# Rope's cosine product on VectorE from PSUM, its closing sum and a softmax subtraction on GpSimd

## The chip, the cores and the metric

The kernel runs on one core of a Trainium2 chip. A core has five engines that take their instructions in order and work beside each other: TensorE (PE in the profile) multiplies matrices from SBUF into PSUM, VectorE (DVE), ScalarE (ACT) and GpSimd (POOL) work on tiles, and SyncE (SP) issues most transfers. They wait for each other by semaphores. The metric is the device time of one execution in microseconds, the median over several runs. Lower is better.

## The reference, cut to what matters

One layer of a decoder trunk with 512 tokens of width 1024. After a norm, one projection gives the inputs of a pooling mixer and of a sparse attention with 16 heads; both are gated, merged and projected, and an MLP of width 4096 follows. Two pieces of the attention are touched here:

```python
def apply_rope(x, cos, sin):
    x1, x2 = jnp.split(x, 2, axis=-1)
    rot = jnp.concatenate([-x2, x1], axis=-1)
    y = x.astype(jnp.float32) * cos[:, None, :] + rot.astype(jnp.float32) * sin[:, None, :]
    return y.astype(x.dtype)
...
    q = apply_rope(q.reshape(B, S, N_HEADS, dh), cos, sin).reshape(B, S, G, HPG, dh)
    ks = apply_rope(ks.reshape(B, S, G, dh), cos, sin)
    kw = apply_rope(kw.reshape(B, S, G, dh), cos, sin)
...
        s_c = jnp.einsum('bqghd,bngd->bghqn', qb, k_cmp) * scale
        p_c = masked_softmax(s_c, cmp_end[None, :] <= t[:, None])
        o_c = jnp.einsum('bghqn,bngd->bqghd', p_c, v_cmp)
```

The first turns pairs of channels by an angle that grows with the position. The second is the softmax over 31 compressed keys for each query, one of three branches of the attention. The other two go over all earlier keys; with 512 tokens every block is picked and the window holds all of them, so both are causal softmaxes over the same positions with different keys and values.

## The kernel before, in words

All matrix products split each float32 operand into a high part and a remainder, and run three products (high by high, high by low, low by high). So every weight that arrives is split: ScalarE writes the high part (line 345), VectorE or, for the second half of a weight in the attention stage, GpSimd subtracts it from the raw weight (line 347).

The work falls into three stages: the projections with the pooling mixer and the compression of keys and values; the attention; and the output projection with the MLP, whose products are made with fewer multiplications by sums of quarters of the weights. Those sums are made by transfers which GpSimd issues (line 267, `S<-w_ff`).

**Rope** (`rope`, line 606) is called ten times: for the two keys (`ks`, `kw`) and for the queries of eight pairs of heads (`q0` to `q7`). ScalarE copies the projected tile from PSUM to `rx` with a scale (line 612). Four transfers on SyncE's queue write `rx` to `rs` with each pair of 32 partitions exchanged (615). Then `rx` is multiplied in place by the cosines in two halves (620), `rs` by the sines in two halves (623), and the two are added into `rx` (628). In the first stage, which holds the keys and q0 to q2, VectorE does all six; in the attention stage (`mode["pool"]`) GpSimd does the four products of q3 to q7 and VectorE the two sums. What follows makes the split operands, for a query in `q_done` (lines 653 to 658). `rope` is a generator: at each `yield` other work is emitted, so the number of yields says how many slots later the next instruction comes.

**The attention** goes pair by pair. A pair has twelve slots; each is one block of scores for one head (half 0: both branches for 128 or 256 positions; half 1: one branch, 384 or 512). For a slot, PE makes scores (`psS`, 1007), VectorE adds the mask, writes `P` and takes the minimum, since the scores are negated (1029), ScalarE takes the exponent with its sum (1039), VectorE inverts the sum (1049), GpSimd scales `P` by that and by the gate (1052), PE transposes `P` (`psT`, 1069), ScalarE and VectorE split the transposed tile (1080, 1084), and PE multiplies it with the values (`psO`, 1103). The transposes of a slot come four slots behind its scores, the product with the values two slots later still. Between slots PE runs filler, the remaining projections (`psF`, 388): q3 to q7 and the gate of the second mixer.

**The compressed branch** (`cmp_scores`, 939) runs as such a generator once for each pair, one pair ahead: scores (`psC`, 944), mask and sum of the two halves on VectorE (951, 952), the minimum (954), its subtraction (956), the exponent on ScalarE (959), the sum, its inverse and the gate on VectorE (961 to 964), then scaling and splitting on GpSimd (966 to 969), the transposes (977), and a copy by ScalarE (`pc`, 979) that PE multiplies into `psO` (1094).

The program text gives only the order of emission. A planner then orders the instructions of each engine by when it holds them to be ready; so instructions of later slots can stand ahead of earlier ones, and a changed instruction moves others.

Of the kernel before, what the change touches and what calls it, by code (L numbers as in the profile page):

```python
# [13 lines left out]
F32 = mybir.dt.float32  # L14
FR = mybir.dt.float32r
AF = mybir.ActivationFunctionType
ALU = mybir.AluOpType
# [3 lines left out]
S = 512  # L21
# [41 lines left out]
def trunk(ctx: ExitStack, tc: tile.TileContext, A, out):  # L63
    nc = tc.nc
    PE, ACT, DVE, POOL = nc.tensor, nc.scalar, nc.vector, nc.gpsimd
    PSUM = bass.MemoryType.PSUM

    def pool(name, **kw):
        return tc.tile_pool(name=name, bufs=1, reuse_waits="tile", **kw)
# [200 lines left out]
    mode = {"pool": False, "first": POOL}  # L270
# [202 lines left out]
    op = e2.enter_context(pool("op"))  # L473
# [3 lines left out]
    ap = at.enter_context(pool("att"))  # L477
# [86 lines left out]
    r, _ = evac0(1)  # L564
# [32 lines left out]
    cosT, sinT = cst[:, C_COS:C_COS + S], cst[:, C_SIN:C_SIN + S]  # L597
# [8 lines left out]
    def rope(ps, scale, done, after=0):  # L606

        assert not scored["rope"]
        scored["rope"] = 1
        xr = ap.tile([128, S], F32, tag="rx", bufs=1, name="rx")  # L610
        sw = ap.tile([128, S], F32, tag="rs", bufs=1, name="rs")
        ACT.activation(xr, ps, AF.Copy, scale=scale)
        for b in range(4):
            a = b ^ 1
            nc.sync.dma_start(sw[32 * b:32 * b + 32, :], xr[32 * a:32 * a + 32, :])
        yield
        eng = POOL if mode["pool"] else DVE
        hs = [slice(0, S // 2), slice(S // 2, S)]
        for c in hs:
            eng.tensor_tensor(xr[:, c], xr[:, c], cosT[:, c], op=ALU.mult)  # L620
            yield
        for c in hs:
            eng.tensor_tensor(sw[:, c], sw[:, c], sinT[:, c], op=ALU.mult)
            yield
        yield
        for c in hs:
            yield
            DVE.tensor_tensor(xr[:, c], xr[:, c], sw[:, c], op=ALU.add)
        while scored["pairs"] < after:
            yield  # L630
        for _ in done(xr):
            yield
        scored["rope"] = 0
# [250 lines left out]
    with ExitStack() as c2:  # L884
# [54 lines left out]
        def cmp_scores(p):  # L939
            g = p // 4  # L940
            ps = ps2.tile([128, NT, 2, 64], F32, tag="S", bufs=S_BANKS, name="psC")
            for qb in range(NT):
                for h in range(2):
                    PE.matmul(ps[:, qb, h, :], Q[p][:, h, 128 * qb:128 * qb + 128], KC[g], start=True, stop=True,
                              skip_group_check=True)
            w = p2.tile([128, NT, 2, 64], F32, tag="cw", bufs=1, name="cw")
            s8 = p2.tile([128, 3, 8], F32, tag="c8", bufs=1, name="c8")
            cm = cst[:, C_CM:C_CM + 128].rearrange("p (q n) -> p q n", q=NT)
            wl = w[:, :, :, 0:32]
            wf = w.rearrange("p q h n -> p (q h) n")[:, :, 0:32]  # L950
            DVE.tensor_tensor(wl, ps[:, :, :, 0:32], cm[:, :, None, :].to_broadcast([128, NT, 2, 32]), op=ALU.add)
            DVE.tensor_tensor(wl, ps[:, :, :, 32:64], wl, op=ALU.add)
            yield
            DVE.tensor_reduce(s8[:, 0, :], wf, axis=AX.X, op=ALU.min)
            yield
            DVE.tensor_tensor(wf, wf, s8[:, 0, :, None].to_broadcast([128, 8, 32]), op=ALU.subtract)
            yield
            yield
            ACT.activation(wl, wl, AF.Exp, scale=-1.0)
            yield  # L960
            DVE.tensor_reduce(s8[:, 1, :], wf, axis=AX.X, op=ALU.add)
            DVE.reciprocal(s8[:, 2, :], s8[:, 1, :])
            r = s8[:, 2, :].rearrange("p (q h) -> p q h", q=NT)
            DVE.tensor_tensor(r, r, GT[:, :, 6 * p:6 * p + 6:3], op=ALU.mult)
            yield
            POOL.tensor_tensor(wl, wl, r[:, :, :, None].to_broadcast([128, NT, 2, 32]), op=ALU.mult)
            pH, pL = (PC[:, :, e, :].rearrange("p q (h n) -> p q h n", h=2) for e in range(2))
            POOL.tensor_scalar(pH, wl, 1.0, 1.0, op0=ALU.mult, op1=ALU.mult)
            POOL.tensor_tensor(pL, wl, pH.bitcast(F32), op=ALU.subtract)
            yield  # L970
            yield
            yield
            yield
            pt = ps2.tile([128, S], F32, tag="T", bufs=T_BANKS, name="psT")
            for qb in range(NT):
                src = PC[:, qb, :, :].rearrange("p e c -> p (e c)")
                PE.transpose(pt[:, 128 * qb:128 * qb + 128].bitcast(FR), src, identR)
            t = p2.tile([128, S], FR, tag="pc", bufs=1, name="pc")
            ACT.activation(t, pt, AF.Copy)
            PTc[p] = t  # L980
# [126 lines left out]
        def o_evac(p, half):  # L1107
# [7 lines left out]
            split_ready()  # L1115

        side.append(cmp_scores(0))
        while 0 not in PTc:
            fill()
# [491 lines left out]
```

## Time and profile before

| | |
|---|---|
| median of 3 runs | 816.38 us (815.37 to 816.65) |
| the profiled execution | 815.44 us, of which 813.5 us are the span from the first to the last instruction |
| PE busy | 789.4 us, 97% of the span |
| DVE, ACT, POOL busy | 610.0 us, 484.8 us, 202.8 us |
| first stage | about 12 to 184 us of the span |
| attention | about 184 to 385 us |
| output projection and MLP | from there to the end |

A timeline row shows the start of an instruction or of a run of equal ones, how long it took, the engine, the line, the operation, the output and its inputs, how many there are (x4), and in brackets how long the engine stood idle before it and which instruction released it. A windows row shows a stretch of the span and the busy time of each engine in it with the number of instructions; PEclk is the share of its full clock that TensorE was granted. A row of groups shows busy time and the mean of one, then the idle time before them. A row of waits shows the total, the number and the longest.

### The profile page before, as it was taken

To read this page: it belongs to the slowest core of one execution; us is meant where nothing else is said; L and a number is where in the kernel's file an instruction comes from. 1 tells how busy PE (TensorE), PEld (TensorE's weight loads), DVE (VectorE), ACT (ScalarE), POOL (GpSimd) and SP (SyncE) were. 2 spreads that over 40 slices of the span, in tenths; PEclk is the share of its full clock that TensorE was granted. 3 is DMA by queue.
4 is the path that set the end of the run, shared out by engine and by line. 5 is a ranking of instruction groups with operands and counts; after the bars stand their busy time and mean duration, and the time that the engine had idled before them with its cause. 6 is when DMAs were issued, how large, how long until landed. Compare 5 with 4: busy or idle time off the path is not lost.

```text
span 813.5 us, 13961 instructions
## 1 busy us (share of the span) xinstructions
PE 789.4 (97%) x5091; PEld 707.8 (87%) x5091; DVE 610.0 (75%) x1199; ACT 484.8 (60%) x961; POOL 202.8 (25%) x269
## 2 busy tenths in 40 slices
PE   8999999998899999999999999999999999999996
PEld 7889878886788888888788899999999999999985
DVE  5796744539979898888565579996899689987823
ACT  6576533327787887899434475944773477346712
POOL 4000000027767867674334100111111100000000
PEclk9999999999999999999999999999999999999999
DMA  9564632357446634553964807999899955455402
GB/s 287 144 170 110 179 92 89 106 157 165 67 128 119 144 78 91 105 131 74 316 155 155 205 3 211 310 242 282 248 267 245 282 167 182 130 157 181 156 1 103
DMA packets 124445, 130.85 MB, mean 161 GB/s; under 512 B 5173, under 2 KB 112217, under 8 KB 124250
## 3 DMA queue, kind: packets, MB, share of 16 engines
q1 hardware_dynamic: 105082, 110.31, 42.6%
q0 software_dynamic: 19008, 18.88, 16.4%
q8 instruction: 40, 0.66, 0.3%
q10 hardware_dynamic: 288, 0.79, 0.3%
q14 instruction: 27, 0.22, 0.1%
HBM read 125.24 MB, written 39.85 MB: 203 GB/s over the span
## 4 chain that ended last, share of the span: by engine, by line
PE 74%; DVE 17%; ACT 4%; issue 3%; DMA 1%; POOL 0%; DVEq 0%; ACTq 0%; POOLq 0%
PE psF L388 22%; PE psB L388 15%; PE psB L1380 13%; PE psB L1496 8%; PE psO L1103 3%; PE psT L1069 3%; PE psS L1007 3%; DVE wl L302 2%; PE psV L388 2%; DVE P L1029 2%; DVE PT L1084 1%; PE psF L445 1%; DVE w3l L302 1%; DMA raw<-w_ff 1%; ACT P L1039 1%
## 5 line engine op out<-in xcount | busy, mean ns | idle before, releaser
L388 PE MATMUL psF<-R,wh 128*128 128x512 f32 x512 | 166.8, 404 | 0.9 <-ACT GB L682 0.6
L300 ACT ACTIVATE wh<-raw 128x1024 fp32r<-128x1024 f32 x66 | 69.8, 1057 | 75.5 <-PE psB L1496 33.4
L345 ACT ACTIVATE wh<-raw 128x512 fp32r<-128x512 f32 (+1 forms) x104 | 62.5, 619 | 84.6 <-PE psF L388 37.5
L388 PEld LDWEIGHTS psF<-R,wh 128*128 128x128 f32 x512 | 92.4, 189 | 18.7 <-ACT GB L682 0.8
L388 PE MATMUL psF<-R,wl 128*128 128x512 f32 x256 | 101.7, 397 | 0.8 <-DVE wl L347 0.8
L1052 POOL TENSOR_SCALAR P<-P,sm,GT 128x128 f32<-128x128 f32 (+3 forms) x128 | 86.0, 705 | 46.4 <-DVE sm L1049 32.2
L302 DVE TENSOR_TENSOR wl<-raw,wh 128x1024 fp32r<-128x1024 f32 x66 | 80.5, 1220 | 17.7 <-ACT wh L300 17.7
L267 POOL DMA_DIRECT2D S<-w_ff x36 | 41.8, 1160 | 191.9 <-DMA S<-w_ff 154.4
L347 DVE TENSOR_TENSOR wl<-raw,wh 128x512 fp32r<-128x512 f32 (+1 forms) x78 | 56.1, 732 | 33.1 <-ACT wh L345 32.7
L1039 ACT ACTIVATE P<-P,sm 128x128 f32<-128x128 f32 (+3 forms) x128 | 71.1, 557 | 11.7 <-DVE sm L1029 10.4
L1029 DVE CUSTOM_DVE_ANT_0 P<-psS,cst 128x128 f32<-128x128 f32 (+3 forms) x128 | 59.6, 483 | 6.2 <-PE psT L1069 4.6
L1380 PE MATMUL psB<-R,wh 128*128 128x256 f32 x352 | 64.1, 282 | 0.0
L347 POOL TENSOR_TENSOR wl<-raw,wh 128x512 fp32r<-128x512 f32 x28 | 39.0, 1398 | 87.5 <-ACT wh L345 85.2
L1084 DVE TENSOR_TENSOR PT<-psT,PT 128x512 fp32r<-128x512 f32 (+2 forms) x96 | 56.6, 594 | 4.1 <-ACT PT L1080 3.0
L388 PEld LDWEIGHTS psF<-R,wl 128*128 128x128 f32 x256 | 48.3, 188 | 11.9 <-DVE wl L347 0.9
L1080 ACT ACTIVATE PT<-psT 128x512 fp32r<-128x512 f32 (+2 forms) x96 | 49.2, 520 | 14.9 <-PE psT L1069 14.0
L1069 PE MATMUL psT<-ident,P 128*128 128x128 f32 x320 | 51.3, 275 | 6.3 <-POOL P L1052 5.0
L300 ACT ACTIVATE w3h<-raw 128x1024 fp32r<-128x1024 f32 x32 | 33.8, 1057 | 38.8 <-PE psB L1496 16.3
L1380 PEld LDWEIGHTS psB<-R,wh 128*128 128x128 f32 x352 | 54.1, 188 | 0.3 <-DVE R L1322 0.2
L1069 PEld LDWEIGHTS psT<-ident,P 128*128 128x128 f32 x320 | 39.6, 141 | 16.8 <-POOL P L1052 7.8
L1380 PE MATMUL psB<-R,wl 128*128 128x256 f32 x176 | 49.5, 281 | 0.0
L302 DVE TENSOR_TENSOR w3l<-raw,w3h 128x1024 fp32r<-128x1024 f32 x32 | 39.0, 1220 | 13.3 <-ACT w3h L300 13.3
(433 smaller groups left out, 2262.6 us busy)
## 6 DMA issues: line engine op xcount, KB each, us to landing
raw<-w_ff SPq DMA_DIRECT2D x56, 512.0 KB, 4.7
S<-w_ff POOLq DMA_DIRECT2D x36, 512.0 KB, 7.6
raw<-S SPq DMA_DIRECT2D x36, 512.0 KB, 5.1
raw<-w_in SPq DMA_DIRECT2D x32, 512.0 KB, 4.0
S<-w_ff SPq DMA_DIRECT2D x28, 512.0 KB, 5.3
S<-S SPq DMA_DIRECT2D x8, 512.0 KB, 7.0
raw<-w_proj_nsa SPq DMA_DIRECT2D x8, 512.0 KB, 4.1
raw<-w_out SPq DMA_DIRECT2D x8, 512.0 KB, 4.6
```

The costliest lines, as they stand in the source:

```text
L300: ACT.activation(h, t, AF.Copy)
L302: DVE.tensor_tensor(l, t, h.bitcast(F32), op=ALU.subtract)
L345: ACT.activation(h[:, sl], t[:, sl], AF.Copy)
L347: eng.tensor_tensor(l[:, sl], t[:, sl], h[:, sl].bitcast(F32), op=ALU.subtract)
L388: PE.matmul(ps, a, b, start=first and j == 0, stop=last and j == n - 1, skip_group_check=True)
L1029: DVE.tensor_tensor_reduce(out=P[:, o:o + n].rearrange("p (a c) -> p a c", c=128), in0=s, in1=m, scale=1.0, scalar=3e38, op0=ALU.add, op1= ...
L1039: last_exp[:] = [ACT.activation(c, c, AF.Exp, bias=sm[:, 0, e:e + 1], scale=-1.0, accum_out=sm[:, 1, e:e + 1])]
L1052: r = POOL.tensor_scalar(P[:, o:o + n], P[:, o:o + n], sm[:, 2, e:e + 1], GT[:, qb, c + e:c + e + 1], op0=ALU.mult, op1=ALU.mult)
L1069: PE.transpose(pt[:, 128 * j:128 * j + 128], P[:, 128 * j:128 * j + 128], ident)
L1084: DVE.tensor_tensor(dL, src, dH.bitcast(F32), op=ALU.subtract)
L1380: PE.matmul(out, w[u][:, k, 128 * f:128 * f + 128], XB[x][v][:, k, :], **kw)
L1496: PE.matmul(out, YB[y][u][:, k, 128 * f:128 * f + 128], w[v][:, k, :], **kw)
```

## The change

In `rope`, the cosine product becomes one instruction on VectorE over all 512 columns, which reads the projected tile in PSUM, scales it and multiplies by the cosines into a new tile `rc`. The sine products stay where they were. The closing sums go from VectorE to the engine of the products, which in the attention stage is GpSimd, and read `rc` instead of `rx`. The slots of the two cosine products stay as empty ones, one empty slot behind the sines goes, and in the attention stage three are added behind the sums. In `cmp_scores`, the subtraction of the minimum goes to GpSimd; two more slots follow it before the exponent, and one more follows the exponent.

```diff
@@ rope
         xr = ap.tile([128, S], F32, tag="rx", bufs=1, name="rx")
         sw = ap.tile([128, S], F32, tag="rs", bufs=1, name="rs")
+        xc = ap.tile([128, S], F32, tag="rc", bufs=1, name="rc")
         ACT.activation(xr, ps, AF.Copy, scale=scale)
         for b in range(4):
             a = b ^ 1
             nc.sync.dma_start(sw[32 * b:32 * b + 32, :], xr[32 * a:32 * a + 32, :])
+        DVE.scalar_tensor_tensor(xc, ps, scale, cosT, op0=ALU.mult, op1=ALU.mult)
         yield
         eng = POOL if mode["pool"] else DVE
         hs = [slice(0, S // 2), slice(S // 2, S)]
-        for c in hs:
-            eng.tensor_tensor(xr[:, c], xr[:, c], cosT[:, c], op=ALU.mult)
-            yield
+        yield
+        yield
         for c in hs:
             eng.tensor_tensor(sw[:, c], sw[:, c], sinT[:, c], op=ALU.mult)
             yield
-        yield
         for c in hs:
             yield
-            DVE.tensor_tensor(xr[:, c], xr[:, c], sw[:, c], op=ALU.add)
+            eng.tensor_tensor(xr[:, c], xc[:, c], sw[:, c], op=ALU.add)
+        if mode["pool"]:
+            for _ in range(3):
+                yield
@@ cmp_scores
             DVE.tensor_reduce(s8[:, 0, :], wf, axis=AX.X, op=ALU.min)
             yield
-            DVE.tensor_tensor(wf, wf, s8[:, 0, :, None].to_broadcast([128, 8, 32]), op=ALU.subtract)
-            yield
-            yield
+            POOL.tensor_tensor(wf, wf, s8[:, 0, :, None].to_broadcast([128, 8, 32]), op=ALU.subtract)
+            for _ in range(4):
+                yield
             ACT.activation(wl, wl, AF.Exp, scale=-1.0)
+            yield
             yield
             DVE.tensor_reduce(s8[:, 1, :], wf, axis=AX.X, op=ALU.add)
```

More of the change, by code (lines that the diff above doesn't have):

```diff
@@ L955, in cmp_scores @@
             yield
-            DVE.tensor_tensor(wf, wf, s8[:, 0, :, None].to_broadcast([128, 8, 32]), op=ALU.subtract)
+            POOL.tensor_tensor(wf, wf, s8[:, 0, :, None].to_broadcast([128, 8, 32]), op=ALU.subtract)
+            for _ in range(4):
+                yield
+            ACT.activation(wl, wl, AF.Exp, scale=-1.0)
             yield
-            yield
-            ACT.activation(wl, wl, AF.Exp, scale=-1.0)
             yield
```

## The prediction

> **What bounds the kernel now.** I read the shares of the engines first, then the busy times stage by stage, then whom PE waits for in the attention, and last the timelines around those waits.
>
> ```profile
> PE 789.4 (97%) x5091; PEld 707.8 (87%) x5091; DVE 610.0 (75%) x1199; ACT 484.8 (60%) x961; POOL 202.8 (25%) x269
> ```
>
> ```profile
> 20.00:184.00 164.00, 163.14 (x811) 136.47 (x810) 100.94 (x200) 77.26 (x144) 6.56 (x11) 1.00 0.48 132
> 184.00:220.00 36.00, 30.11 (x184) 24.84 (x183) 34.79 (x109) 28.31 (x84) 29.73 (x43) 0.97 0.64 124
> 220.00:380.00 160.00, 157.15 (x1005) 137.45 (x1004) 140.12 (x459) 133.09 (x357) 109.10 (x151) 1.00 0.48 105
> ```
>
> PE is the bound, so only PE's idle time and its clock can give a gain. The change adds no matmul. In the first stage PE stands idle 164.00 - 163.14 = 0.9 us; nothing is to be had there. In the first 36 us of the attention it is 5.9 us, and there DVE (34.79) and POOL (29.73) are nearly full. In the next 160 us it is 2.85 us. The views of waits and of PE's timeline name them:
>
> ```profile
> PE psT L1069 <- POOL P L1052: 5.0, 3, 2.4
> ...
> PE psF L388 <- DVE wl L347: 0.8, 1, 0.8
> ```
>
> ```profile
> 194.06 0.44 PE L1069 MATMUL psT<-ident,P 128*128 128x128 f32 x2 [2.17 <-POOL P L1052]
> 194.83 0.44 PE L1069 MATMUL psT<-ident,P 128*128 128x128 f32 x2 [0.33 <-POOL P L1052]
> ...
> 196.82 0.52 PE L1069 MATMUL psT<-ident,P 128*128 128x128 f32 x3 [0.62 <-DVE PT L1084]
> ...
> 217.52 1.21 PE L1069 MATMUL psT<-ident,P 128*128 128x128 f32 x4 [2.45 <-POOL P L1052]
> ```
>
> Two stalls of over 2 us, both of transposes that wait for a `P` scaled by GpSimd. GpSimd's timeline shows what stood ahead of that scaling:
>
> ```profile
> 190.30 1.83 POOL L620 TENSOR_TENSOR rx<-rx,cst 128x256 f32<-128x256 f32 x2
> 191.69 1.79 POOL L623 TENSOR_TENSOR rs<-rs,cst 128x256 f32<-128x256 f32 x2
> 193.08 2.31 POOL L1052 TENSOR_SCALAR P<-P,sm,GT 128x256 f32<-128x256 f32 x3
> ...
> 212.87 1.78 POOL L347 TENSOR_TENSOR wl<-raw,wh 128x512 fp32r<-128x512 f32 x1
> 214.14 1.88 POOL L620 TENSOR_TENSOR rx<-rx,cst 128x256 f32<-128x256 f32 x2
> 215.51 1.18 POOL L623 TENSOR_TENSOR rs<-rs,cst 128x256 f32<-128x256 f32 x1
> 216.22 1.77 POOL L1052 TENSOR_SCALAR P<-P,sm,GT 128x256 f32<-128x256 f32 x2
> 217.46 1.22 POOL L623 TENSOR_TENSOR rs<-rs,cst 128x256 f32<-128x256 f32 x1
> 218.17 1.76 POOL L1052 TENSOR_SCALAR P<-P,sm,GT 128x384 f32<-128x384 f32 x2
> ```
>
> By the starts, a rope product takes GpSimd 0.70 us ((193.08 - 190.30) / 4); the durations overlap. In the first case four products (2.78 us) stand ahead of the scaling, in the second a weight's split, two cosine products and a sine product (216.22 - 212.87 = 3.35 us). DVE is held in the same stretches:
>
> ```profile
> 190.29 4.16 DVE L956 TENSOR_TENSOR cw<-cw,c 128x256 f32<-128x256 f32 x1
> ...
> 214.28 2.78 DVE L956 TENSOR_TENSOR cw<-cw,c 128x256 f32<-128x256 f32 x1
> ```
>
> ```profile
> L956 DVE TENSOR_TENSOR cw<-cw,c 128x256 f32<-128x256 f32 x7 | 9.5, 1361 | 0.0
> ...
> L628 DVE TENSOR_TENSOR rx<-rx,rs 128x256 f32<-128x256 f32 x10 | 6.7, 674 | 0.0
> ...
> L951 DVE TENSOR_TENSOR cw<-psC,cst 128x256 f32<-128x256 f32 x7 | 2.9, 414 | 0.3 <-PE psC L944 0.3
> ```
> The same amount of work with one input in PSUM (951) takes 0.41 us each time on average; the subtraction (956) and rope's sum (628), with both inputs in SBUF, take 9.5 and 6.7 us where 7 x 0.41 and 10 x 0.41 would be 2.9 and 4.1. So 6.6 + 2.6 = 9.2 us of DVE's busy time are waiting that fits GpSimd's streaks: the subtraction that starts at 190.29 ends at 194.45, past four products and the first scaling.
>
> [...]
>
> After the second stall PE's clock falls:
>
> ```profile
> 215.00:220.00 5.00, 2.55 (x9) 1.92 (x9) 4.78 (x9) 2.31 (x7) 4.93 (x8) 0.76 0.60 94
> 220.00:225.00 5.00, 5.00 (x34) 4.56 (x33) 4.05 (x14) 2.68 (x8) 1.54 (x2) 0.90 0.00 0
> ```
>
> With a granted clock of 0.76 and 0.90 it lost 5 x 0.24 + 5 x 0.10 = 1.7 us.
>
> **The change part by part.**
>
> *First stage* (five ropes, all on VectorE): six instructions of 256 columns become one of 512 from PSUM and four of 256. Nearest row for the new one:
>
> ```profile
> L838 DVE SCALAR_TENSOR_TENSOR yd<-psF,pec,yd 128x512 fp32r<-128x512 f32 x4 | 3.0, 751 | 1.6 <-ACT yd L837 1.6
> ```
>
> 0.75 against 2 x 0.41 removed: nothing, beside a PE that is idle 0.9 us in 164. The four transfers keep their number and place in SyncE's queue. The in-place cosine had to wait until they had read `rx`; now the sine waits for their landing, at the same place in the queue. I take 0, and 0.5 us on both sides.
>
> *DVE in the attention*: the seven subtractions and ten sums leave (16.2 us by the rows above, holds included); five new instructions come (5 x 0.75 = 3.75 us). They read PSUM, so no hold is to be expected, and DVE has 12 us less to do. In the planned order the first of them stands ahead of the first slot's minimum, and waits there for ScalarE's copy of the same tile; every slot of the first pair is behind it. That makes the first `P` up to 0.75 us later. GpSimd is still at a weight's split then, which hides some: +0.4, from 0 to 0.75.
>
> *GpSimd in the attention*: two cosine products per rope go and two sums of the same size come, equal at 0.70 each. The subtraction is new, once for each pair; its nearest row is the scaling of the same tile (line 966, shown below with the new wait): 0.62 us. Two fall into the first 36 us, where GpSimd stands idle 36.00 - 29.73 = 6.3 us: +0.5, from 0 to 2 x 0.62 = 1.24. Seven in all lengthen its queue by 4.3 us; past 220 us it is busy 109 of 160, which hides the other five. The sum transfers that GpSimd issues come later by at most that 0.62 us and feed the MLP.
>
> *First stall.* In the planned order the streak ahead of that scaling is two sines and two sums: four products for four. The 2.17 and 0.33 us stay: 0. What DVE was late through the hold goes, and with it the gap at 196.82: -0.6, from 0 to -0.6.
>
> *Second stall.* The order of GpSimd there, by the two programs:
>
> ```
> before: P256 x2, transfer, L347, L620 x2, L623, P256 x2, L623, P384 x2
> after:  P256 x2, transfer, L623, P256 x2, L623, subtraction, sum x2, P384 x2
> ```
>
> The weight's split has moved forward into idle time and the cosines are gone, so only 0.70 of the 3.35 us stay ahead of the scaling, 2.65 less, more than the stall: -2.45, from 0 to -2.45. The half clock follows that stall and goes with it: -1.7, from 0 to -1.7. Next late is P384: two sines, a subtraction and two sums ahead of it take what they replaced, so GpSimd brings it hardly earlier, and PE comes some 4 us earlier; the +0.5 above holds for that.
>
> *The gap of 0.8 us* is a weight's split on DVE with two SBUF inputs, which can be held as before: 0, to 0.8 either way.
>
> *More slots.* A slot lasts some 2 us (96 slots from 184 to 380). A query's split begins two slots later; line 629 lets it start at slot 10 of its count for q3 and line 1130 asks for it at slot 27, so 17 slots hide it. The compressed transposes come three slots later, where `psO` asks for their copy six slots behind: three are left. Before the first slot the loop takes three more steps of filler, which PE doesn't have to make later.
>
> *The new wait on GpSimd.* Behind its own subtraction GpSimd's scaling of the compressed weights waits for ScalarE and VectorE; the first instance in the trace, with idle engines, shows the trip:
>
> ```profile
> 176.63 0.42 ACT L959 ACTIVATE cw<-cw 128x256 f32<-128x256 f32 x1
> ```
>
> ```profile
> 178.09 0.62 POOL L966 TENSOR_TENSOR cw<-cw,c 128x256 f32<-128x256 f32 x1 [4.40 <-DVE c L964]
> ```
>
> 1.46 us. In the third pair nothing stands between the two in GpSimd's queue, in the fourth two scalings, in the seventh one; behind them wait the scalings of slots. In the third pair that would be late by 1.46 and three instructions (966 to 969, 0.6 each by the row above): 3.3 us. The cover there:
>
> ```profile
> 248.46 0.67 POOL L1052 TENSOR_SCALAR P<-P,sm,GT 128x384 f32<-128x384 f32 x1 [1.46 <-DVE sm L1049]
> ```
>
> ```profile
> 253.28 0.49 PE L1069 MATMUL psT<-ident,P 128*128 128x128 f32 x3
> ```
>
> From the end of the scaling to the transposes 253.28 - 249.13 = 4.15 us; 0.9 are left: 0.
>
> **Sum**: -2.45 - 1.7 - 0.6 + 0.4 + 0.5 = -3.85 us. The profiled execution took 815.44 us, 0.94 less than the median of 816.38 (a span of 813.5 and 1.94 around it). Against its own time the sum gives 811.6, against the median 812.5, which I take.
>
> **The rivals.**
>
> *GpSimd still sets the transposes.* P384 waits behind five instructions (3.4 us); PE comes early and stands there instead. If half of the second stall comes back (1.2) and with it the half clock (1.7), 812.5 + 2.9 = 815.4: no difference that counts, since 0.2%, about what a measurement can tell from no change, is 1.6 us. For it: GpSimd is the fullest engine there once DVE is relieved, with 31 us of work. Against: it stood idle 6.3 us.
>
> *The clock falls all the same.* The first stall stays, and only its place in time decides whether a half clock follows it. Then 812.5 + 1.7 = 814.2, still faster. [...]
>
> *GpSimd's own round trip* (the other side): without cover it costs 3.3 us in the third pair, 3.3 - 1.4 in the fourth and 3.3 - 0.7 in the seventh, 7.8 in all: 820.3. It makes the kernel slower than 818.0 when the three covers are below (7.8 - 5.5) / 3 = 0.8 us on average. For it: PE comes earlier, and the planner has moved scalings in every pair. Against: 4.15 us of cover before.
>
> **How the numbers follow.** Forecast 0.48, its own range 810.8 to 814.4 (all gains with no cost and the 0.8 us gap gone; all costs in full and that gap twice); clock 0.14; GpSimd sets 0.18; round trip 0.20. Faster by over 0.2%: 0.48 + 0.14 = 0.62; within: 0.18; slower: 0.20. The range of 809.5 to 818.3 leaves out the upper part of the round trip, and goes below the forecast for the gap of 0.8 us and part of the first stall.
>
> **What would show it.** Right: rope's sum and the subtraction gone from DVE, its new product at about 0.75 us each time; in the first 36 us of the attention PE idle 2.5 to 3.5 us instead of 5.9, with one stall of over 2 us left; PEclk 1.00 behind it. Wrong: a stall of PE on a `P` of 384 columns in the second pair, a low PEclk behind the first stall, or GpSimd idle ahead of line 966's instruction in the third pair with PE standing soon after.

## The result and the profile after

The changed kernel takes 820.76 us (median of 4 runs, 820.52 to 821.53), the kernel before 815.88 us in the same comparison (4 runs, 815.30 to 816.65): 1.0063 times as long, 95% interval 1.005 to 1.0075. It is slower by 4.9 us; the forecast was 812.5 us, and the time lies outside of the range of 809.5 to 818.3. The profiled execution took 820.6 us with a span of 818.6. The shares of the engines in it:

```profile
PE 790.7 (97%) x5091; PEld 707.2 (86%) x5091; DVE 601.1 (73%) x1181; ACT 483.8 (59%) x961; POOL 207.3 (25%) x277
```

The two stretches of the attention, from the windows view:

```profile
184.00:220.00 36.00, 32.01 (x204) 26.67 (x205) 29.34 (x113) 29.02 (x87) 32.11 (x47) 1.00 0.59 105
220.00:380.00 160.00, 150.48 (x945) 130.69 (x944) 129.85 (x428) 125.77 (x339) 109.26 (x152) 0.99 0.48 104
```

VectorE is relieved (601.1 against 610.0 us in all, 29.34 against 34.79 in the first stretch). In the first stretch PE is idle 4.0 us instead of 5.9 and keeps its full clock. In the second it is idle 9.5 us instead of 2.85. The waits view for the attention and PE's timeline say where:

```profile
PE psT L1073 <- ACT pc L983: 5.0, 3, 3.1
```

```profile
193.06 0.96 PE L1073 MATMUL psT<-ident,P 128*128 128x128 f32 x4 [1.82 <-POOL P L1056]
...
217.15 0.38 PE L1107 MATMUL psO<-PT,VV 128*128 128x256 f32 x1 [1.44 <-ACT PT L1084]
229.21 0.50 PE L388 MATMUL psF<-R,wl 128*128 128x512 f32 x1 [0.78 <-DVE wl L347]
...
245.69 0.41 PE L1073 MATMUL psT<-ident,P 128*128 128x128 f32 x2 [3.05 <-ACT pc L983]
...
295.71 0.51 PE L981 MATMUL psT<-identR,PC 128*128 128x128 f32 x4 [0.98 <-DVE PT L1088]
...
324.10 0.41 PE L1073 MATMUL psT<-ident,P 128*128 128x128 f32 x2 [1.60 <-ACT pc L983]
333.91 0.63 PE L1073 MATMUL psT<-ident,P 128*128 128x128 f32 x4 [0.87 <-POOL wl L347]
```

(Line numbers after the change are 3 higher behind rope and 4 higher behind `cmp_scores`: transposes 1073, GpSimd's scaling 1056, the copies of the transposed tile 1084 and 1088, `pc` 983, the subtraction 959, the compressed exponent 962, the copy that begins a query's split 656.)

How far each program has come is seen from matmuls that both have. Before the change, the scores of the sixth and the ninth slot of the third pair, and the first product of the last stage, start at:

```profile
244.79 0.34 PE L1007 MATMUL psS<-KH,Q 128*128 128x384 f32 x1
...
249.19 0.42 PE L1007 MATMUL psS<-KH,Q 128*128 128x384 f32 x1
...
395.24 0.70 PE L388 MATMUL psB<-R,wh 128*128 128x512 f32 x2 [1.66 <-ACT mH L1280]
```

and after it:

```profile
240.61 0.33 PE L1011 MATMUL psS<-KH,Q 128*128 128x384 f32 x1
...
250.18 0.42 PE L1011 MATMUL psS<-KH,Q 128*128 128x384 f32 x1
...
400.58 0.70 PE L388 MATMUL psB<-R,wh 128*128 128x512 f32 x2 [1.67 <-ACT mH L1284]
```

So the changed kernel is 4.2 us ahead (244.79 - 240.61), falls 1.0 us behind within three slots (250.18 - 249.19), and loses 4.3 us more by the last stage (5.3 behind). Most of these 4.3 us are idle PE too: from the ninth slot to the gap ahead of the last stage PE is idle 5.9 us, before the change 2.1 us (windows of 250.18 to 398.91 and of 249.19 to 393.58 us), and the rows at 295.71, 324.10 and 333.91 are the largest of it. From there to the end of the span both take the same, 818.6 - 400.58 = 418.0 and 813.5 - 395.24 = 418.3 us.

Nearly all of the loss of 5.2 us in three slots is one chain. VectorE, GpSimd and ScalarE there:

```profile
240.65 0.42 DVE L957 TENSOR_REDUCE c<-cw 128x8 f32<-128x256 f32 x1
```

```profile
237.60 1.89 POOL L624 TENSOR_TENSOR rs<-rs,cst 128x256 f32<-128x256 f32 x2
238.99 1.73 POOL L347 TENSOR_TENSOR wl<-raw,wh 128x512 fp32r<-128x512 f32 x1
240.24 1.86 POOL L628 TENSOR_TENSOR rx<-rc,rs 128x256 f32<-128x256 f32 x2
241.65 2.12 POOL L1056 TENSOR_SCALAR P<-P,sm,GT 128x256 f32<-128x256 f32 x3
243.36 0.98 POOL L959 TENSOR_TENSOR cw<-cw,c 128x256 f32<-128x256 f32 x1
```

```profile
244.38 0.42 ACT L962 ACTIVATE cw<-cw 128x256 f32<-128x256 f32 x1 [4.36 <-POOL cw L959]
244.70 0.37 ACT L1084 ACTIVATE PT<-psT 128x256 fp32r<-128x256 f32 x1
244.96 0.59 ACT L983 ACTIVATE pc<-psT 128x512 fp32r<-128x512 f32 x1
```

```profile
240.00:245.00 5.00, 2.64 (x19) 2.08 (x17) 1.78 (x8) 0.64 (x4) 4.34 (x7) 1.00 1.18 291
245.00:250.00 5.00, 4.30 (x18) 3.75 (x19) 2.42 (x10) 2.94 (x8) 3.79 (x6) 0.66 0.02 7
```

The minimum is there at 241.07. The subtraction stands in GpSimd's queue behind rope's sines, a weight's split, rope's two sums and three scalings, and starts at 243.36. ScalarE has the exponent at the head of its queue and does nothing for 4.36 us: 1.05 us until the minimum is there, 2.29 us in which the subtraction waits in GpSimd's queue, and 0.98 us for the subtraction. Behind the exponent stand the two copies that would free the two `psT` banks. PE waits 3.05 us for a bank, and then runs at a granted clock of 0.66, which costs 5 x 0.34 = 1.7 us. That makes 4.75 us; the other 0.4 us are work, four compressed transposes (241.09 to 241.47 on PE) that the kernel before had made ahead of its sixth slot. So of the lead of 4.2 us, too, 0.4 us were work still to be done.

### The profile page after: what moved, and what is told of

Same layout as the page of the kernel before. It is cut to its first block, busy times and chain, and to the rows that moved or that the text cites. A ratio compares the mean times of both kernels' runs of the same rounds, so it can differ in the third digit from the quotient of the medians.

```text
span 818.6 us, 13957 instructions
## 1 busy us (share of the span) xinstructions
PE 790.7 (97%) x5091; PEld 707.2 (86%) x5091; DVE 601.1 (73%) x1181; ACT 483.8 (59%) x961; POOL 207.3 (25%) x277
## 3 DMA queue, kind: packets, MB, share of 16 engines
q0 software_dynamic: 19008, 18.88, 16.3%
## 4 chain that ended last, share of the span: by engine, by line
PE 67%; DVE 15%; ACT 7%; POOL 5%; issue 4%; DMA 1%; ACTq 0%; POOLq 0%; DVEq 0%
PE psF L388 20%; PE psB L388 15%; PE psB L1384 13%; PE psB L1500 7%; DVE wl L302 2%; PE psO L1107 2%; PE psT L1073 2%; POOL P L1056 2%; PE psV L388 2%; ACT P L1043 1%; PE psS L1011 1%; DVE P L1033 1%; PE psF L445 1%; DVE w3l L302 1%; DMA raw<-w_ff 1%
## 5 line engine op out<-in xcount | busy, mean ns | idle before, releaser
L300 ACT ACTIVATE w3h<-raw 128x1024 fp32r<-128x1024 f32 x32 | 33.8, 1057 | 38.2 <-PE psB L1500 16.3
L1107 PE MATMUL psO<-PT,VV 128*128 128x256 f32 x320 | 49.2, 289 | 1.7 <-ACT PT L1084 1.7
```

Of the source, the lines that this page charges most:

```text
L300: ACT.activation(h, t, AF.Copy)
L1107: PE.matmul(ps[:, qb % 2, :, :], VV[:, k, b, g, :], t[:, j, :, :], start=False, stop=last and j == len(kbs) - 1 and t is tL, skip_group_ch ...
```

## The experiments

Ratios are to the kernel before, with 95% intervals. It was run again beside each group of kernels (medians of 815.07 to 816.71 us), so the ratios are to be compared and not the times. The diffs of kernels 1 to 4 and 8 are against the changed kernel, the others against the kernel named. "ScalarE's wait" adds up, from the waits view for the stretch of 184 to 400 us, how long ScalarE stood at a compressed exponent or at a query's copy whose input was late; for the kernel before and the changed one:

```profile
ACT cw L959 <- DVE cw L956: 4.8, 2, 3.3
ACT Q L653 <- DVE rx L628: 0.2, 1, 0.2
```

```profile
ACT cw L962 <- POOL cw L959: 13.1, 7, 4.4
ACT Q L656 <- POOL rx L628: 3.8, 2, 2.1
```

| | rope's work in the attention | subtraction | us | ratio | ScalarE's wait, us |
|---|---|---|---|---|---|
| before | cosines, sines on GpSimd | VectorE | 815.88 | 1 | 5.0 |
| changed | sines, sum on GpSimd | GpSimd, slots | 820.76 | 1.0063 (1.0050 to 1.0075) | 16.9 |
| 1 | as changed | GpSimd, transposes early | 820.81 | 1.0049 (1.0031 to 1.0068) | 14.6 |
| 2 | as changed | VectorE, slots | 821.43 | 1.0060 (1.0038 to 1.0082) | 11.1 |
| 3 | as changed | GpSimd, no slots | 819.43 | 1.0043 (1.0023 to 1.0063) | 16.3 |
| 4 | as changed | VectorE, no slots | 822.40 | 1.0071 (1.0055 to 1.0088) | 10.5 |
| 5 | as before | GpSimd, slots | 822.60 | 1.0088 (1.0071 to 1.0105) | 5.1 |
| 6 | as before | GpSimd, no slots | 821.71 | 1.0077 (1.0057 to 1.0098) | 8.4 |
| 7 | sines on GpSimd | VectorE | 812.23 | 0.9959 (0.9945 to 0.9974) | 0.9 |
| 8 | sines on GpSimd | GpSimd, slots | 815.07 | 0.9995 (0.9985 to 1.0004) | 5.6 |
| 9 | sines on GpSimd | GpSimd, no slots | 818.30 | 1.0042 (1.0027 to 1.0057) | 7.6 |
| 10 | none on GpSimd | VectorE | 809.03 | 0.9929 (0.9914 to 0.9944) | 1.0 |
| 11 | as before, three empty slots | VectorE | 817.40 | 1.0031 (1.0020 to 1.0043) | 5.2 |
| 12 | as changed, six slots | VectorE | 820.40 | 1.0074 (1.0050 to 1.0097) | 11.9 |
| 13 | none on GpSimd | GpSimd, slots | 809.46 | 0.9924 (0.9909 to 0.9940) | 4.1 |
| 14 | none on GpSimd, no slots | VectorE | 810.61 | 0.9931 (0.9910 to 0.9952) | 1.6 |
| 15 | none on GpSimd, full width | VectorE | 807.53 | 0.9892 (0.9873 to 0.9910) | 0.6 |

**1. The transposes as early as before.**

```diff
             POOL.tensor_tensor(pL, wl, pH.bitcast(F32), op=ALU.subtract)
             yield
-            yield
-            yield
-            yield
             pt = ps2.tile(...)
```

> The changed kernel, but three of the four empty slots between the GpSimd split of the compressed probabilities and their transposes are taken away, so the transposes come no later in the source than before the change; subtraction and sum stay on GpSimd. Theory A (the extra slots carry ScalarE's copy pc of one pair behind the next pair's exponent, which waits for GpSimd, and the transposes of P find no bank): the stall of 3.05 us at 245.69 and those of 0.39 and 1.60 us that end on pc are gone, with the half clock behind them; about 6 us less than the changed kernel, 813 to 815.5 us. Theory B (an exponent that waits for GpSimd holds ScalarE and all behind it, wherever pc stands): ScalarE still waits some 13 us in all for the subtraction and its other work is as late; 819 to 821 us. Theory C (rope on the two engines is the loss): 819 to 821 us too, with no stall on pc.

820.81 us. No stall on `pc` is left, and nothing is gained: there are new ones of 1.60 us for GpSimd's split of the compressed weights and of 1.78, 1.13, 1.04 and 0.84 us behind late work on VectorE. Theory A falls: the place of `pc` decided where PE stood, not how long in all.

**2. The slots without the move.**

```diff
-            POOL.tensor_tensor(wf, wf, s8[:, 0, :, None]..., op=ALU.subtract)
+            DVE.tensor_tensor(wf, wf, s8[:, 0, :, None]..., op=ALU.subtract)
             for _ in range(4):
```

> The changed kernel with the compressed scores' subtraction back on VectorE, the extra slots kept. ScalarE's order is that of the changed kernel (pc right behind the next pair's exponent in pair three). Theory A: the late copy remains but the exponent no longer waits for GpSimd, only for VectorE; the 3.05 us stall shrinks to under 1 us unless GpSimd's rope holds VectorE's subtraction again; 815 to 818 us. Theory B: the whole loss goes; 812 to 814 us. Theory C: 819 to 821 us.

821.43 us, just above what theory C expects and far from A and B. With the subtraction back on VectorE the whole loss is still there.

**3. The move without the slots.**

```diff
             POOL.tensor_tensor(wf, wf, s8[:, 0, :, None]..., op=ALU.subtract)
-            for _ in range(4):
-                yield
+            yield
+            yield
             ACT.activation(wl, wl, AF.Exp, scale=-1.0)
             yield
-            yield
```

> The changed kernel with the subtraction on GpSimd but the slots as before the change (one before and one after the exponent, three fewer in all). Theory A: pc stands ten places and more ahead of the next exponent again, no stall on pc; the exponent waits longer for GpSimd since it has three slots less; 814 to 817 us. Theory B: more waiting of ScalarE for GpSimd than the 13.1 us of the changed kernel, 821 to 824 us. Theory C: 819 to 821 us.

819.43 us: within theory C's range. With or without the slots ScalarE waits 13.1 us for the subtraction in the attention.

**4. Rope's part alone** (the compressed part as before the change).

```diff
-            POOL.tensor_tensor(wf, wf, s8[:, 0, :, None]..., op=ALU.subtract)
-            for _ in range(4):
-                yield
+            DVE.tensor_tensor(wf, wf, s8[:, 0, :, None]..., op=ALU.subtract)
+            yield
+            yield
             ACT.activation(wl, wl, AF.Exp, scale=-1.0)
-            yield
             yield
```

> Rope's part of the change alone: cosines on VectorE, closing sum on GpSimd, its slots as changed; the compressed scores wholly as before the change. Theories A and B: no stall on pc after 220 us; the loss is gone, and what the first 36 us of the pair loop give depends on whether GpSimd's four rope instructions, now products and sums, still hold VectorE's subtraction (4.16 us before the change); 813 to 816 us. Theory C: most of the loss of 4.9 us stays; 819 to 821 us.

822.40 us, 1.4 us above theory C's range; rope's part alone loses as much as the whole change. VectorE's subtraction, back on its engine, is held for longer than before the change:

```profile
190.09 4.56 DVE L959 TENSOR_TENSOR cw<-cw,c 128x256 f32<-128x256 f32 x1
215.29 4.25 DVE L959 TENSOR_TENSOR cw<-cw,c 128x256 f32<-128x256 f32 x1
```

and GpSimd's sum makes ScalarE wait, VectorE behind it, and PE behind that (ScalarE's, VectorE's and PE's timelines):

```profile
284.98 0.63 ACT L656 ACTIVATE Q<-rx 64x512 fp32r<-64x512 f32 x1 [1.71 <-POOL rx L628]
```

```profile
285.64 0.69 DVE L659 TENSOR_TENSOR Q<-rx,Q 64x512 fp32r<-64x512 f32 x1 [1.42 <-ACT Q L656]
```

```profile
288.55 0.52 PE L1072 MATMUL psT<-ident,P 128*128 128x128 f32 x3 [1.61 <-DVE PT L1087]
```

**5 and 6. The compressed part alone, and of it the subtraction alone.** Against the kernel before; 5 has the whole diff below, 6 its first two lines:

```diff
-            DVE.tensor_tensor(wf, wf, s8[:, 0, :, None]..., op=ALU.subtract)
+            POOL.tensor_tensor(wf, wf, s8[:, 0, :, None]..., op=ALU.subtract)
-            yield
-            yield
+            for _ in range(4):
+                yield
             ACT.activation(wl, wl, AF.Exp, scale=-1.0)
+            yield
```

> The kernel before with the compressed scores' part of the change alone: subtraction on GpSimd, three more slots, rope as before the change. Theory C (rope's part is the loss, the subtraction the gain): the stalls in the first 36 us of the pair loop shrink as in the changed kernel, start of the third stage 3 to 5 us earlier than the changed kernel's; 811 to 816.5 us. Theory A (extra slots) still expects a stall of 2 us or more on pc with half clock behind it, since exponent and pc stand side by side in pair three here too: 816 to 820 us.

> The kernel before with one word changed: the compressed scores' subtraction runs on GpSimd; no slots added, rope as before the change. Theory C: the long hold of VectorE (4.16 and 2.78 us) is gone, some 2 to 4 us are gained in the first two pairs, nothing is lost later; 811.5 to 815 us. Theory B (an exponent that waits for GpSimd holds ScalarE) expects the gain to be given back in the later pairs; 816 to 820 us.

822.60 and 821.71 us, slower by 0.88 and 0.77%. I had expected a gain from both, and theory C as I put it falls: each part alone loses about as much as both together (1.0071 and 1.0088 against 1.0063; the intervals overlap, and the differences are no larger than what the empty slots of 11 make). In 6 theory B is nearer (ScalarE waits 8.4 us, all for the subtraction), though 821.71 is above its range too; in 5 the time is above both ranges. With the subtraction gone from VectorE, the next instruction there that has two inputs in SBUF is held in its place, rope's own sum (5's VectorE):

```profile
190.83 3.50 DVE L628 TENSOR_TENSOR rx<-rx,rs 128x256 f32<-128x256 f32 x2 [1.84 <-POOL rs L623]
...
243.22 3.12 DVE L628 TENSOR_TENSOR rx<-rx,rs 128x256 f32<-128x256 f32 x1
```

where the kernel before had 1.03 us for two and 0.74 for one. In the third pair PE pays for it, behind a copy that VectorE makes right after (PE's timeline; 1070 and 1085 are the transposes and the copy that stood at 1069 and 1084):

```profile
247.97 0.64 PE L1070 MATMUL psT<-ident,P 128*128 128x128 f32 x2 [2.63 <-DVE PT L1085]
```

**7. The cosines alone: kernel 4 with the sum back on VectorE. 8. The changed kernel with the sum back.** The same line in both:

```diff
-            eng.tensor_tensor(xr[:, c], xc[:, c], sw[:, c], op=ALU.add)
+            DVE.tensor_tensor(xr[:, c], xc[:, c], sw[:, c], op=ALU.add)
```

> Rope's cosines on VectorE from PSUM as in the change, but the closing sum on VectorE again; rope's slots as changed, compressed scores as before the change. Theory C1 (the closing sum on GpSimd makes ScalarE's copy of Q wait at the head of its queue, VectorE's low part behind it, and the transposes behind that): the stalls of 1.61 and 0.44 us near 289 us of the rope-alone run go, with the half clock behind; start of the third stage 2.5 to 4 us earlier than the 399.96 us of the rope-alone run; 815 to 818 us. Theory C2 (the new product on VectorE or rope's shifted slots are the loss): as rope alone, 819 to 822 us.

> The changed kernel with only the closing sum of rope back on VectorE. Theory C1: 815 to 818 us; GpSimd's queue is shorter by 1.4 us ahead of the subtraction of pair three, so the 3.05 us stall at 245.69 shrinks by about that, and falls below the gap that is followed by half clock. Theory C2: 819 to 822 us.

812.23 us, faster than the kernel before and better than either theory, and 815.07 us, no difference from before, with no stall on `pc` in the third pair. The length of a gap does not tell whether half clock follows it: 2.45 us before the change was followed by it, 2.54 us in kernel 4 was not. C1 has the right sign, and less than the size in 7: the closing sum on GpSimd costs 0.9959 to 1.0071, 1.1% or 9 us, with the subtraction on VectorE, and 0.9995 to 1.0063, 0.7% or 5.5 us, with it on GpSimd. In 7 GpSimd has two rope products in a row, not four, and VectorE's subtraction is held less. But the hold is not gone: rope's sum just ahead of it takes 2.83 us for two, while GpSimd runs three scalings of `P` (190.68 to 192.92):

```profile
190.38 2.83 DVE L628 TENSOR_TENSOR rx<-rc,rs 128x256 f32<-128x256 f32 x2 [0.52 <-POOL rs L624]
193.13 0.41 DVE L959 TENSOR_TENSOR cw<-cw,c 128x256 f32<-128x256 f32 x1
213.42 2.00 DVE L959 TENSOR_TENSOR cw<-cw,c 128x256 f32<-128x256 f32 x1
```

**9. Kernel 7 with the subtraction on GpSimd, no slots.**

```diff
-            DVE.tensor_tensor(wf, wf, s8[:, 0, :, None]..., op=ALU.subtract)
+            POOL.tensor_tensor(wf, wf, s8[:, 0, :, None]..., op=ALU.subtract)
```

> Cosines on VectorE, the closing sum on VectorE, the compressed scores' subtraction on GpSimd without the added slots: against the run with the cosines alone (812.23 us) the subtraction's engine is the only difference. Theory S (ScalarE's exponent waits for GpSimd at the head of its queue, so the subtraction on GpSimd costs by itself): 815 to 819 us. Theory D (its only cost is in the added slots): 811.5 to 813 us.

818.30 us: theory S. One instruction per pair, on another engine, costs 0.9959 to 1.0042, 0.8% or 6.8 us. ScalarE waits for it 7.6 us (six times), where it waited 0.9 us (once) in 7.

**10. Nothing of rope on GpSimd.** Against 7:

```diff
-        eng = POOL if mode["pool"] else DVE
+        eng = DVE
```

> Cosines, sines and closing sum of rope all on VectorE in the attention too, compressed scores as before the change: GpSimd has nothing of rope. Theory H (VectorE's subtraction with both inputs in SBUF is held until a streak of GpSimd's work ends, and rope's instructions make the streaks): the subtraction takes 0.41 to 1.4 us in all seven pairs, with no instance of 2 us; the time depends on whether VectorE has room for two more products for each rope, 811 to 815 us. Rival (the hold comes from anything that GpSimd does, the scalings of P above all): an instance of 2 us or more stays, 813 to 818 us.

809.03 us, 0.71% faster than before. The subtraction on VectorE takes at most 0.526 us (the view of its line), and PE is idle 0.1 us in the first 36 us (its windows row):

```profile
L959 DVE TENSOR_TENSOR cw<-cw,c x7: 404/415/526, 190.7 to 336.5; 128x256 f32<-128x256 f32 x7
```

```profile
184.00:220.00 36.00, 35.89 (x229) 30.57 (x228) 34.78 (x128) 30.49 (x90) 27.23 (x39) 1.00 0.58 110
```

Theory H holds for the subtraction: without rope on GpSimd it is not held any more, though GpSimd still scales every `P`. Other instructions of VectorE with two inputs in SBUF still are at times: its split of a weight (line 347), which takes 0.69 us at 182.36, takes 1.66 us at 270.94, beside a split by GpSimd from 270.75 to 272.05 (VectorE's and GpSimd's timelines). VectorE makes 15 more instructions for the five queries in the attention (five products of 512 columns, ten of 256) in no more busy time than before the change (34.78 against 34.79 us in the first stretch, 609.8 against 610.0 us in all): what it had spent on being held pays for them.

**11. Three empty slots, no operation moved.** Against the kernel before, behind rope's sum:

```diff
+        if mode["pool"]:
+            for _ in range(3):
+                yield
```

> The kernel before with nothing but three empty slots added behind rope's closing sum in the attention, as the change has them; every operation stays on its engine. Theories S and H: no stall is added, 814.5 to 817 us. Theory N (any edit moves the planned order, and that alone is worth several us either way): outside of 813 to 818.5 us.

817.40 us, 0.31% slower: 0.4 us above what theories S and H expect, and not outside of the bounds that theory N names. The planned order alone can be worth some 2 us, so differences of this size between the other kernels prove nothing about engines.

**12. Kernel 4 with six empty slots behind the sum.**

```diff
-            for _ in range(3):
+            for _ in range(6):
                 yield
```

> The rope part alone with six empty slots behind the closing sum on GpSimd instead of three. Theory S (the loss of that run lies in ScalarE's copy of Q, which waits for GpSimd's sum at the head of its queue): ScalarE no longer waits for the sum (3.2 us over two times before), the stalls of 1.61 and 0.44 us near 289 us go with the half clock; about 3 us less than 822.4 us, 817.5 to 820.5. Theory H alone (the loss is the long hold of VectorE's subtraction in the first two pairs, 4.56 and 4.25 us, against 0.41 and 2.00 with the cosines alone): the holds stay and the time too, 821 to 823.5 us.

820.40 us, by its ratio no other than kernel 4 (1.0074 against 1.0071). It does not decide, since the slots did not do what they were for: ScalarE's wait for GpSimd's sum grew from 3.2 to 4.7 us (two times each).

**13. Kernel 10 with the compressed part as changed** (the diff of 5).

> Rope wholly on VectorE in the attention (809.03 us as measured), and the compressed scores' part as changed: subtraction on GpSimd, three more slots. Theory Q (the subtraction costs because it comes behind rope's instructions in GpSimd's queue): ScalarE's exponent waits under 5 us in all for GpSimd, against 13.1 us for the seven in the changed kernel, and the time stays within 2 us of the run without it: 808 to 811 us. Theory T (the trip over GpSimd costs, whatever else GpSimd has): 5 to 7 us more, as from the cosines alone (812.23) to the cosines with the subtraction (818.3): 814 to 816 us.

809.46 us, a ratio of 0.9924 against 0.9929 without: theory Q. The trip over GpSimd is no measurable cost when GpSimd's queue is free of rope, although ScalarE waits 4.1 us for it against 1.0 in kernel 10; the same edit costs 0.9% from the kernel before to 5 and 0.4% from 7 to 8, where it comes behind rope's instructions. In the third pair GpSimd now waits for the minimum and starts at once, and ScalarE has no idle time ahead of the exponent (GpSimd's and ScalarE's timelines):

```profile
238.16 0.62 POOL L959 TENSOR_TENSOR cw<-cw,c 128x256 f32<-128x256 f32 x1 [1.43 <-DVE c L957]
```

```profile
239.14 0.40 ACT L962 ACTIVATE cw<-cw 128x256 f32<-128x256 f32 x1
```

**14. Kernel 10 without the three empty slots. 15. Kernel 10 with sines and sum in one instruction each.** The first diff is 14, the second 15:

```diff
-        if mode["pool"]:
-            for _ in range(3):
-                yield
```

```diff
-        hs = [slice(0, S // 2), slice(S // 2, S)]
+        hs = [slice(0, S)]
...
-            for _ in range(3):
+            for _ in range(6):
```

> Rope wholly on VectorE as in the run of 809.03 us, without the three empty slots behind its sum; no operation changes its engine. It measures what the planned order alone is worth near the fastest kernel. If the null run's 2.3 us (817.4 against 815.07) is typical of a shifted order: 806.5 to 811.5 us; if that was a chance: 808.5 to 809.5 us. No theory of engines expects more than 1 us.

> Rope wholly on VectorE as in the run of 809.03 us, with the sines and the sum made as one instruction of 512 columns each instead of two of 256 (0.68 us against 2 x 0.41 by the rows of the new product and the subtraction), 0.28 us less of VectorE for each rope, 1.4 us for the five in the attention; slots kept in number. VectorE is the engine that PE waits for there, so up to 1 us: 807.5 to 810 us; an order that falls worse costs up to 2 us more.

14 has the ratio of 10 (0.9931 against 0.9929), so the 2 us of the null run are not a rule, though the intervals leave room for 0.2% either way. 15 is the fastest kernel, 807.53 us, 1.1% faster than before (in the attention a rope passes eleven slots behind its transfers, one more than in 10, so their number was not quite kept):

```profile
184.00:220.00 36.00, 35.44 (x226) 30.32 (x226) 34.09 (x124) 30.63 (x90) 26.27 (x37) 1.00 0.61 117
220.00:380.00 160.00, 158.62 (x1010) 137.27 (x1009) 141.01 (x457) 137.44 (x364) 105.12 (x140) 1.00 0.51 115
```

PE is idle 0.6 and 1.4 us in the two stretches, 5.9 and 2.85 before. That is more than the 1 us I had expected of the wider instructions; with an order that can be worth some 2 us, how much of it is the width stays open.

## Why the prediction was wrong

**What held.** In the stretch that the sum was made for, its total came out: -3.85 us were predicted, and the sixth slot of the third pair starts 4.18 us earlier, 3.8 without the work still to be done. Part of that is luck, since the terms under it did not come out one by one. The second stall was to go whole (-2.45); instead PE stands 0.21 us there for GpSimd's `P` and then 1.44 us for a copy by ScalarE, so only 0.8 us are gained. The first stall was to stay (0); it is 1.82 us instead of 2.17 and 0.33, so 0.68 are gained. The gap at 196.82 is 0.27 instead of 0.62, the clock behind the second stall is full, the gap of 0.8 us stayed at 0.78. PE is idle 4.0 us in the first 36 us, not 2.5 to 3.5, and no stall of over 2 us is left there. The new product on VectorE takes 0.68 us where 0.75 was taken.

**What failed.** Two steps that the sum put at nothing: the wait on GpSimd for the moved subtraction, and the swap of products for sums on GpSimd. The experiments weigh the second more: putting the sum alone back on VectorE takes the whole loss away (8, 0.9995), putting the subtraction alone back takes none of it away (2 and 4, 1.0060 and 1.0071). Each costs by itself as well (4 and 9, each against 7), and the two do not add up.

**"The new wait on GpSimd", 0.** The step asked who waits behind GpSimd's scaling of the compressed weights, found 4.15 us of cover against 3.3, and stopped there. It did not ask who waits for the subtraction itself: ScalarE's exponent, which holds ScalarE's whole queue. In the third pair that came to 4.36 us on ScalarE, 3.05 on PE and 1.7 by the clock; over the seven pairs ScalarE stood 13.1 us. Before the change the exponent stood 4.8 us. The rows were there: the subtraction was going to join a queue in which a weight's split and three rope instructions take 3.35 us, and the exponent (line 959 before the change) was the first thing behind it.

**"GpSimd in the attention": two products go and two sums come, equal.** By time on GpSimd they are. But the cosine products had the whole of rope to hide in, and the sum is rope's last step, for which ScalarE's copy of the query waits at the head of its queue (3.8 us) and VectorE behind that. Kernels 7 and 8, which put the sum alone back, price that swap at 9 and 5.5 us. VectorE's 8.9 us of busy time that the change took away (610.0 - 601.1) were no gain in all.

**"More slots", 0.** Here the step named the right place and the wrong neighbour. The compressed transposes come three slots later and still reach `psO` in time, as counted; but their copy now stands in ScalarE's queue behind the next pair's exponent. Kernel 1 shows that this alone is not the loss: with the copy early again, PE stands elsewhere for as long.

**The rivals.** "GpSimd's own round trip" gave 820.3 us, 0.5 from the measured time, with a chance of 0.20. Its sign and its engine were right and its place was not, so the near hit is luck: it put the stalls behind the scaling of the compressed weights. In the third pair GpSimd does stand idle ahead of that scaling (1.69 us, line 970, at 246.03), as the sign of this rival said, but PE has no gap of 0.2 us from then until 263.66. The mechanism that happened is one step earlier in the same trip. "GpSimd still sets the transposes" is seen only as the 1.82 us of the first stall; "the clock falls all the same" did not happen behind the first stall (PEclk 1.00 from 184 to 220 us), but behind a new one (0.66 behind the gap of 3.05 us). The place in time that it goes by is seen before the change and in kernel 4, where stalls of 2.17 and 2.54 us kept the full clock (last section).

**What the runs put in its place.** One cause fits most of the table: GpSimd works through rope, and the scalings behind it, in streaks, and whoever needs something at such a time waits for the end of the streak. VectorE waits with instructions that have two inputs in SBUF (4.16 us before, 4.56 in kernel 4, 3.12 for another instruction in kernel 5); an instruction that is moved to GpSimd to escape that waits in its queue (2.29 us in the third pair of the changed kernel), and ScalarE with it (4.36 us). The change moved two of VectorE's held instructions into the queue that held them. Taking rope off GpSimd shortens both waits (10 and 15), and then it no longer matters to the time where the subtraction is made (13). What this does not explain is why each part of the change alone (4 and 5) costs as much as both together, and how much of each ratio is the planned order, of which 11 shows 0.3% and 14 none; the step from 7 to 10, the sines alone, is 0.3% too. ScalarE's wait is not the measure of the loss: kernel 5 waits no longer than the kernel before and is 0.9% slower, where PE stands behind VectorE's held sum; kernel 13 waits 4.1 us and is as fast as 10.

## What to carry to other kernels

When an instruction is moved to another engine, price its consumer too: the instruction that waits for it stands at the head of its engine's queue, and all behind it waits as well (here ScalarE did nothing for 4.36 us, with the copies of two `psT` banks behind the exponent), so count what is ahead of the moved instruction in its new queue at the moment when its input is ready. If an engine is late because another one holds it (here VectorE, 4.16 us for a subtraction of 0.41), shorten the other one's streak rather than hand it more work: here the rope of five queries on VectorE, its cosines read from PSUM, gave 0.7 to 1.1%, where handing VectorE's work to GpSimd lost 0.6%. Before a difference of a few tenths of a per cent is put down to a cause, run the same program with a few empty slots added and nothing moved.

## What the runs showed of the hardware

The hold of VectorE is not limited to one instruction of GpSimd's: in kernel 4 the subtraction stands from 190.09 to 194.65 us, while GpSimd runs four rope instructions and three scalings, and ends 0.3 us after GpSimd pauses (GpSimd's timeline; the next scaling starts at 195.51):

```profile
189.59 1.78 POOL L624 TENSOR_TENSOR rs<-rs,cst 128x256 f32<-128x256 f32 x2
190.97 1.74 POOL L628 TENSOR_TENSOR rx<-rc,rs 128x256 f32<-128x256 f32 x2
192.37 2.00 POOL L1055 TENSOR_SCALAR P<-P,sm,GT 128x256 f32<-128x256 f32 x3
```

What is held is seen from the views of the lines. Before the change the subtraction and rope's sum, with both inputs in SBUF, take 0.41 to 4.16 us (956, eight times) and 0.40 to 1.55 us (628, twenty times); the addition in line 951, of the same size and with one input in PSUM, takes 0.41 to 0.43 us in all its eight instances, and the new product after the change, which reads PSUM too, 0.67 to 0.69 us in all ten. In kernel 10, with rope off GpSimd, the subtraction takes 0.526 us at most.

TensorE's clock went to half behind gaps of 0.78 to 3.05 us each. By PEclk in the windows of the traces, a stretch at half in the attention lasts 3.4 us before and after the change and in kernels 4, 9 and 10, and in kernel 5 one lasts 3.4 us and one 6.9 us; the two of kernel 4 begin 95.6 us apart, 28 times 3.41 us. Before the change, in windows of 3.41 us laid so that one of them is the stretch at half:

```profile
190.31:193.72 3.41, 1.58 (x10) 1.06 (x8) 3.41 (x2) 0.81 (x3) 3.41 (x7) 1.00 0.73 86
193.72:197.13 3.41, 2.12 (x12) 1.39 (x12) 3.41 (x8) 1.72 (x4) 2.34 (x4) 1.00 0.44 70
214.20:217.61 3.41, 0.96 (x8) 0.64 (x7) 3.40 (x4) 1.88 (x5) 3.41 (x7) 1.00 1.04 147
217.61:221.02 3.41, 3.41 (x13) 2.84 (x14) 3.10 (x10) 2.00 (x5) 2.91 (x5) 0.50 0.04 7
```

The first stall, 2.17 us from 191.89, is cut by the border at 193.72, which leaves PE 1.83 us idle in the first window, and the full clock follows; the second stall lies in the third window, 2.45 us idle, and the clock behind it is 0.50. After the change it is 0.50 from 246.56 to 249.97, behind a window with 2.55 us idle. In kernel 10, PE's timeline and two windows laid in the same way:

```profile
227.11 0.30 PE L1072 MATMUL psT<-ident,P 128*128 128x128 f32 x1 [0.78 <-ACT pc L982]
228.42 0.79 PE L388 MATMUL psF<-R,wl 128*128 128x512 f32 x1 [1.01 <-DVE wl L347]
```

```profile
225.02:228.43 3.41, 1.62 (x11) 1.07 (x9) 3.35 (x7) 2.25 (x8) 2.44 (x2) 1.00 0.00 0
228.43:231.84 3.41, 3.41 (x8) 2.73 (x9) 2.84 (x13) 1.83 (x8) 1.27 (x3) 0.50 0.66 178
```

The two gaps add up to 1.79 us within one window, and the clock is 0.50 in the next. In kernel 4 a gap of 2.54 us is cut by the border at 218.69, which leaves 1.75 us of it in the window behind, and the full clock follows:

```profile
220.44 0.47 PE L1097 MATMUL psO<-pc,VC 128*128 128x256 f32 x2 [2.54 <-DVE oT L1115]
```

```profile
218.69:222.10 3.41, 1.66 (x12) 1.64 (x13) 3.37 (x8) 1.72 (x4) 1.86 (x3) 1.00 0.28 44
222.10:225.51 3.41, 3.41 (x25) 2.92 (x23) 2.83 (x14) 2.70 (x8) 1.54 (x2) 1.00 0.01 2
```

So the two near gaps of kernel 10 (0.78 and 1.01 us) were followed by the half clock, and the longer gaps of 2.54 us in kernel 4 and of 2.17 us before the change were not. This bears on the forecast's term for the half clock: it came out, but the length of one gap does not give it, nor does the idle time in such a window alone (1.79 us with the half clock behind it, 1.83 us without), and the clock is not the same in each execution: the four of kernel 6 have mean clocks of 0.991 to 0.997.
